# A hybrid decoder layer on one core: order of the first loads, a longer warm-up, and eight chunks at once for the first half of the tokens at the last gate

## The chip, the cores and the metric

The kernel runs on one core of a Trainium2 chip. The metric is the time of one execution on the device in microseconds (us). The kernel before has a median of 2290.51 us over 3 runs (2288.47 to 2292.35). One profiled execution of it took 2290.02 us, of which 2288.2 us are the span that the profile shows.

The engines: TensorE (PE in the profile) multiplies matrices, VectorE (DVE) and ScalarE (ACT) work on elements, SyncE (SP) issues transfers and computes nothing. ACT can issue transfers too. DMA engines move data between HBM and the on-chip memory SBUF. TensorE writes into PSUM, eight banks of 128 x 512 float32.

## What is computed

One decoder layer for 256 tokens of width 2048, in float32, cut to what matters here:

```python
h = layer_norm(alpha * x + 0.5 * swiglu(x, w_ffn1_gu, w_ffn1_down))      # first half-FFN
h = layer_norm(alpha * h + mixers(h))                                     # retention and windowed attention
h = layer_norm(alpha * h + 0.5 * swiglu(h, w_ffn2_gu, w_ffn2_down))      # second half-FFN
ple = sigmoid(h @ w_ple_gate) * (p @ w_ple_proj)                          # the last gate
out = layer_norm(alpha * h + ple)
def swiglu(x, w_gu, w_down):
    g, u = split(x @ w_gu, 2)
    return (silu(g) * u) @ w_down
```

The change touches the very first loads of the first half-FFN, and the seam between the second half-FFN (its last products with `w_ffn2_down`, then the layer norm) and the product with `w_ple_gate`, called the last gate below. In the kernel that weight is `w_pg`.

## The kernel before, in words

**Numbers in two parts.** Each float32 operand is split into a high part, rounded to the TensorE's float32r type by a copy on ACT, and a low part, the difference, made by DVE. The helper `split` (lines 92 to 94) does this. A product of two operands is three matmuls, low x high, high x high, high x low (`Sum.add`, lines 292 to 302).

**Chunks of weights.** Weights come in chunks of 512 KB, 128 x 1024 elements. A chunk needs a transfer into a raw buffer (`Chunk.__init__`, line 107), a copy on ACT (line 93) and a subtraction on DVE (line 94). The raw buffer is free after that, and the two parts are held until TensorE has used them. A chunk holds two blocks of 128 rows and 512 columns. Used for all 256 tokens it takes 12 matmuls: two halves of the tokens, t=0 and t=1, two row blocks, three matmuls each. This text calls the six matmuls of one chunk for one half of the tokens a *step*, and three of them, one row block, a *half-step*.

**The planner.** All chunks stand in `plan` in the order of their use. `fill()` (line 186), called whenever a chunk has been used, issues transfers (`load`) and conversions (`make`) for coming chunks. It makes the next loaded chunk while the chunks that are made and waiting amount to less than `room["ahead"]` (a chunk of this kind counts 12), loads while made and loaded ones amount to less than `room["far"]`, and does neither beyond `room["slots"]` buffers. `quiet(True)` stops conversions. All this happens when the program is written: it fixes the order of instructions on each engine, and every engine works in its order.

**The buffers.** Chunks, their parts, columns of the residual and other tiles of up to 4 KB a partition come from one pool of 46 buffers (`SLOTS`). An instruction that writes a new tile waits until the last reader of the buffer's previous tile is done. The framework hands buffers out in program order, and takes for each new tile the buffer that comes free first by its own plan.

**The end of the second half-FFN.** `ffn("f2", 2, ...)` works through the last half of the output columns in 19 units, plain pairs of chunks and units of seven products (`Seven`). After the last unit of seven, DVE folds four sums (`seven_common`, lines 405 to 408, then line 858). Six chunks, three each for output columns 2 and 3, are kept for the end: `held_out` runs their six steps for t=0, then their twelve half-steps for t=1. After the third step `Norm.columns` (in the profile as L907 and L539) adds a block to the residual and takes its statistics; after the sixth `Norm.normal(0)` does so for the last block, works out mean and variance and normalizes the first 512 columns of t=0 (lines 510 and 511). The rest of the norm is spread out: `turn((t, c))` normalizes columns c+1, transposes columns c on TensorE (line 518) and splits them into `ht`, the input of the last gate. Events (count, what) say after which half-step or step that happens; "sums" is `normal(1)`, the same for t=1.

**The last gate.** `embedding` multiplies `ht` with `w_pg` in four blocks of 512 columns, eight chunks each. Chunk c needs rows 2c and 2c+1 of `ht`, so two chunks for each `turn`. In block 0, `Norm.first` runs six chunks (`FRONT`) for t=0, then the same six for t=1, then two more for both halves. The four `ppr` tiles, p times its projection, are fetched at the start of the gate.

**The start.** `warm_up` has TensorE transpose the identity 14 times. `load_x_chunk(0)` issues the first quarter of x in three parts on SP, then the first two chunks of weights in two pieces each, one on ACT's queue, one on SP's.

The functions that the diff touches and what calls them, with the profile's line numbers:

Of the kernel before, what the change touches and what calls it, by code (L numbers as in the profile page):

```python
# [25 lines left out]
KD = D // P  # L26
# [3 lines left out]
HELD_MIX = 4  # L30
FRONT = 6

WARM = 14
FRONT_PAIRS = 3
HELD_PAIRS = 2, 3
SLOTS = 46
# [14 lines left out]
def layer(ctx: ExitStack, tc: tile.TileContext, io):  # L51
    nc = tc.nc
    sync, act, dve, pool, pe = nc.sync, nc.scalar, nc.vector, nc.gpsimd, nc.tensor
# [11 lines left out]
    def banks(name):  # L65
        return [bank(name + str(j)) for j in range(2)]

    def slot(shape, dt, name):
        return slots.tile(shape, dt, tag="slot", name=name)
# [116 lines left out]
    def fill(must=False):  # L186

        while True:
            queued = sum(u.time for u in ready)
            left = room["slots"] - room["used"]  # L190
            wanted = must and not ready or not room["quiet"] and queued < room["ahead"]
            if loaded and wanted and loaded[0].makes <= left:
                u = loaded.pop(0)
                u.make()
                room["used"] += u.keeps - u.loads
                ready.append(u)
                continue
            first = loaded[0] if loaded else plan[0] if plan else None
            queued += sum(u.time for u in loaded)
            if plan and queued < room["far"] and plan[0].loads + first.makes <= left:  # L200
                u = plan.pop(0)
                u.load()
                room["used"] += u.loads
                loaded.append(u)
                continue
            return
# [8 lines left out]
    def take(key):  # L215
        if not ready:
            fill(True)
        u = ready.pop(0)
        assert u.key == key, (u.key, key)
        return u  # L220

    def done(u):
        room["used"] -= u.keeps
        fill()

    def slots_for_weights(n, ahead=45, far=90):
        room.update(slots=n, ahead=ahead, far=far)
# [76 lines left out]
    def half_of(a, t):  # L304
        return tuple(x[:, t * P : (t + 1) * P] for x in a)

    def tokens_chunk(chunk, k0, lhs, sums, ts, kks=(0, 1)):
        for kk in kks:
            for t in ts:
                sums[t].add(half_of(lhs(k0 + kk), t), chunk.columns(kk))  # L310
# [419 lines left out]
    def gu_keys(name, j):  # L730
        return lambda n, p: (name + "_gu", j, n, p)
# [15 lines left out]
    def down_keys(name, b):  # L747
        return lambda n, p: (name + "_down", 2 * b + n, p)
# [9 lines left out]
    def ffn(name, i, ht, norm, keep, residual, keepers, away):  # L758
# [28 lines left out]
        for j in range(KF // 4):  # L787
# [9 lines left out]
            sums = [[Sum((pg, pu)[n][t], n_of[t, n]) for n in range(2)] for t in range(2)]  # L797
            got = []

            if norm is not None and j == 0:  # L800
                front, units = units[:FRONT_PAIRS], units[FRONT_PAIRS:]
                steps = [(gu_keys(name, 0)(n, p), 2 * p, n) for _, p in front for n in range(2)]
# [41 lines left out]
        lhs = lambda k: tuple(a[:, k % 4, :] for a in acts[k // 4])  # L844
# [9 lines left out]
        def fold(b):  # L854
            def f(*a):
                e, w = seven_common(*a)
                for x, v in ((y[2 * b], e), (y[2 * b + 1], w)):
                    dve.scalar_tensor_tensor(x, x, 2.0 * ALPHA, v, ALU.mult, ALU.add)
            return f
# [16 lines left out]
        sums = [[Sum(pn[n][t], n_of[0][t, n]) for n in range(2)] for t in range(2)]  # L876
# [5 lines left out]
            block_stats(stats, y, n)  # L882


        last_ahead = 136
        last = {}
        for at, (kind, p) in enumerate(second + [("P", p) for p in held]):
            last[p // 2] = at
# [11 lines left out]
        pt_ = [banks(f"{name}e{t}") for t in range(2)]  # L900
        sums = [[Sum(pt_[t][n], n_of[1][t, n]) for n in range(2)] for t in range(2)]
        block(f"{name}d1", second, down_keys(name, 1), lhs, forms, sums, fold(1), before_unit)
        slots_for_weights(27, last_ahead, last_ahead + 24)
        steps = [(down_keys(name, 1)(n, p), 2 * p, n) for n in range(2) for p in held]

        def combine(sl, p):
# [2 lines left out]
        norm = Norm((2, 3), sums, combine, y, stats, i, 4 * LN_EPS, keepers, away)  # L909
        if i < 2:  # L910
            events = ((8, (0, 0)), (10, (0, 1)), (11, (0, 2)), (12, "make"), (12, "make"), (12, "sums"))
            norm.run(steps, lhs, events, (0, 1), 4)
        else:
            norm.run(steps, lhs, ((8, (0, 0)), (11, (0, 1))))
        return norm


# [415 lines left out]
    def embedding(ht, norm, y):  # L1333
        stats = small.tile([P, 2, 4, 6], F32, tag="stats", name="plst", bufs=1)

        def finish(blk, ps, sg, t):
            sl = y[blk][:, t]
            act.activation(sg[:, t], ps, AF.Sigmoid)
            dve.tensor_tensor(sg[:, t], sg[:, t], pp[blk][:, t], ALU.mult)
            dve.scalar_tensor_tensor(sl, sl, ALPHA, sg[:, t], ALU.mult, ALU.add)  # L1340
            dve.bn_stats(stats[:, t, blk, :], sl)

        def last_norm(t, mv, rstd):
            rows = io["out"][0, t * P : (t + 1) * P]
            for c in range(4):
                ln_normal(y, t, mv, rstd, g, b, 4 * c, 4)
                at = slice(c * 512, c * 512 + 512)
                (act if t and c % 2 else sync).dma_start(rows[:, at], y[c][:, t])

        lhs = lambda k: (ht[:, k, :S], ht[:, k, S:])  # L1350
        for blk in range(4):
            pgs = banks(f"pg{blk}")
            sums = [Sum(b, KD) for b in pgs]
            sg = slot([P, 2, 512], F32, f"sg{blk}")
            key = ("w_pg", blk)
            if blk == 0:
                for j in range(4):
                    pp[j] = load_columns(pp, j, "ppr")
                steps = [(key + (c,), 2 * c, 0) for c in range(FRONT)]
                norm.first(steps, lhs, [[s] for s in sums], (  # L1360
                    (1, (0, 2)), (1, "sums"), (6, (1, 0)), (7, (1, 1)), (8, (0, 3)), (9, (1, 2)),
                    (10, (1, 3)), (10, "go"),
                ))
                slots_for_weights(24)
                for c in range(FRONT, KD // 2):
                    u = take(key + (c,))
                    tokens_chunk(u.chunk, 2 * c, lhs, sums, (0, 1))
                    done(u)
            elif blk < 3:
                for c in range(KD // 2):  # L1370
                    u = take(key + (c,))
                    tokens_chunk(u.chunk, 2 * c, lhs, sums, (0, 1))
                    done(u)
                    run_side()
            if blk < 3:
                finish(blk, pgs[0], sg, 0)
                later(1, lambda blk=blk, pgs=pgs, sg=sg: finish(blk, pgs[1], sg, 1))
                if blk == 0:
                    g, b = ln_vectors(3)
                continue  # L1380

            def first_done():
                finish(3, pgs[0], sg, 0)
                last_norm(0, *ln_stats(stats[:, 0], 3, 0, LN_EPS))

            steps = [(key + (c,), 2 * c, 0) for c in range(KD // 2)]
            held_out(steps, lhs, [[s] for s in sums], lambda t, j: None, first_done, lambda n: None, 0)
            finish(3, pgs[1], sg, 1)
            last_norm(1, *ln_stats(stats[:, 1], 3, 1, LN_EPS))
# [11 lines left out]
    def load_x_chunk(c):  # L1401
        raw = slot([P, 4, S], F32, f"xraw{c}")
        x_parts[c] = raw
        if c:
            sync.dma_start(raw, io["xT"][c])
            split_x(c, slice(0, 4))
            return
        parts = [slice(0, 1), slice(1, 2), slice(2, 4)]
        for at in parts:
            sync.dma_start(raw[:, at], io["xT"][c][:, at])  # L1410
        for queue in (act, sync):
            u = plan.pop(0)
            u.load(pieces=2, queue=queue)
            u.chunk.make_hi()
            room["used"] += u.keeps
            ready.append(u)
        first, second = (u.chunk for u in ready)
        split_x(c, parts[0])
        first.make_part(first.parts[0])
        split_x(c, parts[1])  # L1420
        first.make_part(first.parts[1])
        for at in second.parts:
            second.make_part(at)
        split_x(c, parts[2])

    def split_x(c, at):
        to = ht[:, 4 * c : 4 * c + 4, :][:, at]
        split(to[:, :, :S], to[:, :, S:], x_parts[c][:, at])

    def warm_up():  # L1430

        ps = bank("warm")
        for _ in range(WARM):
            pe.transpose(ps[:, :P], ident, ident)

    with tc.manual_schedule():
# [12 lines left out]
        norm = ffn("f1", 0, ht, None, x_parts, x_columns, (), rows[0])  # L1449
        norm = mixers(norm.new, norm, rows[0], kept, rows[1])  # L1450
        norm = ffn("f2", 2, norm.new, norm, norm.keep, rows[1], (), None)
# [102 lines left out]
```

## Time and profile before

| | us |
|---|---|
| median of 3 runs | 2290.51 |
| the runs | 2288.47, 2292.35, 2290.51 |
| the profiled execution | 2290.02 |
| its span | 2288.2 |
| TensorE busy in the span | 2268.8 (99%) |
| DVE busy | 1945.7 (85%) |
| ACT busy | 1184.7 (52%) |
| DMA, mean over the span | 204 GB/s |

A line of the timeline gives the start in us from the beginning of the span, the duration, the engine, the line of the kernel, what is written and read, and how many instructions are merged into it. In brackets stands how long the engine was idle before, and what released it. "SPq" and "ACTq" are issues of transfers; their time is that of the issue, not of the transfer. Starts of successive matmuls overlap: what counts is the distance from one start to the next.

### The profile page before, as it was taken

The numbers are of one execution on the slowest core, as the hardware profiler recorded it, in microseconds if no ns is written. First come the engines' busy times: TensorE is split into PE (matmuls) and PEld (weight loads), VectorE is DVE, ScalarE is ACT, GpSimd is POOL, SyncE is SP. The second block draws the span as 40 slices with busy tenths as digits, with TensorE's granted clock in tenths as the row PEclk, the third lists the DMA queues.
The fourth block names the chain that finished last, engine by engine and source line by source line (L and its number), as shares of the span: only waits on it lengthen the run. The fifth ranks groups of instructions, "written<-read, shape, count | busy, mean of one in ns | idle before, by whom it ended". The sixth has DMA issues, their size and how long they took to land.

```text
span 2288.2 us, 28790 instructions
## 1 busy us (share of the span) xinstructions
PE 2268.8 (99%) x10480; PEld 1883.5 (82%) x10480; DVE 1945.7 (85%) x2468; ACT 1184.7 (52%) x1427; POOL 95.5 (4%) x53
## 2 busy tenths in 40 slices
PE   9999999999999999999999999999999999999997
PEld 7888888888888888888778888888888888888876
DVE  7899999999888785677789786779999999889877
ACT  6555555556554342435556454355565555555532
POOL 0000000000000530124000000000000000000000
PEclk9999999999999999999999999999999999999999
DMA  8666665665577565555447567576666566565771
GB/s 298 199 206 195 198 211 180 206 200 192 214 279 278 179 222 169 166 165 163 140 150 243 167 224 274 190 233 206 197 189 208 184 201 216 181 220 194 276 276 55
DMA packets 193997, 465.83 MB, mean 204 GB/s; under 512 B 14784, under 2 KB 16448, under 8 KB 193856
## 3 DMA queue, kind: packets, MB, share of 16 engines
q1 hardware_dynamic: 191584, 460.91, 61.1%
q10 hardware_dynamic: 2272, 3.10, 0.5%
q8 instruction: 82, 1.34, 0.2%
q14 instruction: 59, 0.48, 0.1%
HBM read 455.56 MB, written 8.39 MB: 203 GB/s over the span
## 4 chain that ended last, share of the span: by engine, by line
PE 96%; DVE 3%; DMA 1%; issue 0%; ACT 0%; DVEq 0%; ACTq 0%
PE f1g L300 3%; PE f1g L302 3%; PE f1g L301 3%; PE f2g L302 3%; PE f2g L300 3%; PE f2g L301 3%; PE rqk L251 3%; PE f1u L300 2%; PE f1u L302 2%; PE f1u L301 2%; PE f2u L302 2%; PE f2u L300 2%; PE f2u L301 2%; PE aqk L251 2%; PE f2d L300 2%; PE f1d L300 2%
## 5 line engine op out<-in xcount | busy, mean ns | idle before, releaser
L94 DVE TENSOR_TENSOR lf_gu<-rf_gu,hf_gu 128x1024 fp32r<-128x1024 f32 (+1 forms) x284 | 334.5, 1212 | 14.4 <-ACT hf_gu L93 13.5
L93 ACT CAST hf_gu<-rf_gu 128x1024 fp32r<-128x1024 f32 (+1 forms) x284 | 282.3, 1043 | 18.8 <-DMA rf_gu<-in_f_gu 18.5
L94 DVE TENSOR_TENSOR lw_in_f<-rw_in_f,hw_in_f 128x1024 fp32r<-128x1024 f32 x140 | 195.7, 1428 | 29.4 <-ACT hw_in_f L93 26.8
L94 DVE TENSOR_TENSOR lf_down<-rf_down,hf_down 128x1024 fp32r<-128x1024 f32 x152 | 181.3, 1221 | 22.2 <-ACT hf_down L93 19.2
L93 ACT CAST hf_down<-rf_down 128x1024 fp32r<-128x1024 f32 x152 | 155.3, 1051 | 75.2 <-DMA rf_down<-in_f_down 21.4
L93 ACT CAST huf_gu<-uf_gu 128x1024 fp32r<-128x1024 f32 x70 | 73.7, 1054 | 158.0 <-DVE uf_gu L166 158.0
L93 ACT CAST hw_in_f<-rw_in_f 128x1024 fp32r<-128x1024 f32 x140 | 138.8, 1051 | 2.9 <-DMA rw_in_f<-in_w_in_f 2.7
L300 PE MATMUL f1g<-hf_gu,xt 128*128 128x512 f32 x247 | 97.2, 394 | 0.7 <-ACT hf_gu L93 0.7
L302 PE MATMUL f1g<-lf_gu,xt 128*128 128x512 f32 x247 | 97.1, 393 | 0.0
L301 PE MATMUL f1g<-hf_gu,xt 128*128 128x512 f32 x247 | 97.0, 393 | 0.0
L300 PE MATMUL f2g<-hf_gu,ht 128*128 128x512 f32 x247 | 96.3, 390 | 0.0
L302 PE MATMUL f2g<-lf_gu,ht 128*128 128x512 f32 x247 | 96.2, 389 | 0.0
L301 PE MATMUL f2g<-hf_gu,ht 128*128 128x512 f32 x247 | 96.1, 389 | 0.0
L93 ACT CAST hvf_gu<-vf_gu 128x1024 fp32r<-128x1024 f32 x70 | 73.8, 1055 | 29.7 <-DVE vf_gu L168 29.5
L829 ACT ACTIVATE eve<-eve 128x1024 f32<-128x1024 f32 x20 | 21.2, 1061 | 124.5 <-DVE eve L828 124.5
L94 DVE TENSOR_TENSOR luf_gu<-uf_gu,huf_gu 128x1024 fp32r<-128x1024 f32 x70 | 85.3, 1219 | 0.0
L94 DVE TENSOR_TENSOR lvf_gu<-vf_gu,hvf_gu 128x1024 fp32r<-128x1024 f32 x70 | 85.3, 1219 | 0.0
L300 PE MATMUL f2u<-hf_gu,ht 128*128 128x512 f32 x212 | 83.7, 395 | 0.0
L300 PE MATMUL f1u<-hf_gu,xt 128*128 128x512 f32 x212 | 83.4, 394 | 0.0
L302 PE MATMUL f2u<-lf_gu,ht 128*128 128x512 f32 x212 | 82.6, 390 | 0.0
L301 PE MATMUL f2u<-hf_gu,ht 128*128 128x512 f32 x212 | 82.6, 389 | 0.0
L301 PE MATMUL f1u<-hf_gu,xt 128*128 128x512 f32 x212 | 82.5, 389 | 0.0
(1336 smaller groups left out, 6432.0 us busy)
## 6 DMA issues: line engine op xcount, KB each, us to landing
rf_gu<-in_f_gu SPq DMA_DIRECT2D x350, 512.0 KB, 4.9
rf_down<-in_f_down SPq DMA_DIRECT2D x176, 512.0 KB, 4.4
rw_in_f<-in_w_in_f SPq DMA_DIRECT2D x148, 512.0 KB, 4.4
rw_rv<-in_w_rv SPq DMA_DIRECT2D x32, 512.0 KB, 4.5
rw_ret<-in_w_ret SPq DMA_DIRECT2D x32, 512.0 KB, 4.7
rw_mix<-in_w_mix SPq DMA_DIRECT2D x32, 512.0 KB, 4.4
rw_pg<-in_w_pg SPq DMA_DIRECT2D x32, 512.0 KB, 4.6
rw_att<-in_w_att SPq DMA_DIRECT2D x16, 512.0 KB, 4.6
```

The source lines that it names most:

```text
L93: act.copy(dst_hi, src)
L94: (lo_engine or dve).tensor_tensor(dst_lo, src, dst_hi, ALU.subtract)
L251: pe.matmul(ps[f], hi[:, kk, f * P : (f + 1) * P], rhs(k), start=k == 0, stop=k == n_k - 1,)
L300: pe.matmul(o, al, bh, start=first, stop=False)
L301: pe.matmul(o, ah, bh, start=False, stop=False)
L302: pe.matmul(o, ah, bl, start=False, stop=self.left == 0)
L829: act.activation(g, g, AF.Silu)
```

## The change

There are four edits. (1) At the start both first chunks of weights go on SP's queue, in the order chunk 0, chunk 1; the first two parts of x go on ACT's queue, the third on SP's behind the weights. (2) `WARM` goes from 14 to 17. (3) In the second half-FFN alone, `last_ahead` goes from 136 to 160 and the slots at the held chunks from 27 to 31, and `turn((0, 0))` and `turn((0, 1))` come after half-steps 9 and 12 in place of 8 and 11. (4) Block 0 of the last gate runs all eight chunks for t=0 and then all eight for t=1; the events are moved accordingly, and `turn((0, 3))` now comes before "sums".

```diff
-WARM = 14
+WARM = 17
...
-        last_ahead = 136
+        last_ahead, n_ahead = (136, 27) if i < 2 else (160, 31)
...
-        slots_for_weights(27, last_ahead, last_ahead + 24)
+        slots_for_weights(n_ahead, last_ahead, last_ahead + 24)
...
-            norm.run(steps, lhs, ((8, (0, 0)), (11, (0, 1))))
+            norm.run(steps, lhs, ((9, (0, 0)), (12, (0, 1))))
...
-                steps = [(key + (c,), 2 * c, 0) for c in range(FRONT)]
+                steps = [(key + (c,), 2 * c, 0) for c in range(KD // 2)]
                 norm.first(steps, lhs, [[s] for s in sums], (
-                    (1, (0, 2)), (1, "sums"), (6, (1, 0)), (7, (1, 1)), (8, (0, 3)), (9, (1, 2)),
-                    (10, (1, 3)), (10, "go"),
+                    (1, (0, 2)), (2, (0, 3)), (2, "sums"), (7, (1, 0)), (9, (1, 1)), (11, (1, 2)),
+                    (12, (1, 3)), (12, "go"),
                 ))
                 slots_for_weights(24)
-                for c in range(FRONT, KD // 2):
-                    u = take(key + (c,))
-                    tokens_chunk(u.chunk, 2 * c, lhs, sums, (0, 1))
-                    done(u)
...
         parts = [slice(0, 1), slice(1, 2), slice(2, 4)]
-        for at in parts:
-            sync.dma_start(raw[:, at], io["xT"][c][:, at])
-        for queue in (act, sync):
+        for j in range(2):
             u = plan.pop(0)
-            u.load(pieces=2, queue=queue)
+            u.load(pieces=2, queue=sync)
             u.chunk.make_hi()
             room["used"] += u.keeps
             ready.append(u)
+            for at in (parts[:2], parts[2:])[j]:
+                (sync if j else act).dma_start(raw[:, at], io["xT"][c][:, at])
```

## The prediction

> **What bounds the kernel now.** I read the page first, then what TensorE waited for, then the timeline of the two places that the change touches.
>
> ```profile
> PE 2268.8 (99%) x10480; PEld 1883.5 (82%) x10480; DVE 1945.7 (85%) x2468; ACT 1184.7 (52%) x1427; POOL 95.5 (4%) x53
> ```
>
> TensorE is the bound. All its waits of the whole execution fit in one answer:
>
> ```profile
> PE warm L1434 <- POOL ident masks.py:199: 1.4, 1, 1.4
> PE pg L300 <- DVE ht L94: 1.3, 1, 1.3
> PE lnps L518 <- DVE f1y L511: 1.0, 2, 0.5
> PE f1g L300 <- ACT hf_gu L93: 0.7, 1, 0.7
> PE lnps L518 <- DVE f2y L511: 0.5, 2, 0.3
> PE lnps L518 <- DVE mixy L511: 0.3, 1, 0.3
> ```
>
> The change can reach 0.7 (first matmul) and 1.3 + 0.5 (last gate): 2.5 us of waits. The timeline of TensorE at the start adds a slow clock:
>
> ```profile
> 1.36 3.25 PE L1434 MATMUL warm<-ident 128*128 128x128 f32 x14 [1.36 <-POOL ident masks.py:199]
> 5.28 0.79 PE L300 MATMUL f1g<-hf_gu,xt 128*128 128x512 f32 x1 [0.67 <-ACT hf_gu L93]
> ...
> 9.71 0.63 PE L301 MATMUL f1g<-hf_gu,xt 128*128 128x512 f32 x1
> 10.14 0.63 PE L302 MATMUL f1g<-lf_gu,xt 128*128 128x512 f32 x1
> 10.56 0.46 PE L300 MATMUL f1u<-hf_gu,xt 128*128 128x512 f32 x1
> 10.86 0.39 PE L301 MATMUL f1u<-hf_gu,xt 128*128 128x512 f32 x1
> ```
>
> Matmuls start 0.427 apart until 10.56, then 0.227: half speed, and full speed from about 10.73 (the step between the last two lines, 0.30, mixes both).
>
> At the last gate DVE sets the pace. Its timeline, the six conversions of gate chunks 0 to 5 behind it, and two starts on TensorE:
>
> ```profile
> 2166.03 1.22 DVE L858 SCALAR_TENSOR_TENSOR f2y<-f2y,evw 128x1024 f32<-128x1024 f32 x1
> 2167.16 4.66 DVE L94 TENSOR_TENSOR lw_pg<-rw_pg,hw_pg 128x1024 fp32r<-128x1024 f32 x4
> 2171.74 0.68 DVE L907 TENSOR_TENSOR f2y<-f2y,f2e 128x512 f32<-128x512 f32 x1
> ...
> 2177.88 0.48 DVE L511 SCALAR_TENSOR_TENSOR f2y<-f2y,rstd,ln_b 128x256 f32<-128x256 f32 x1
> ...
> 2178.42 0.44 PE L518 MATMUL lnps<-ident,f2y 128*128 128x128 f32 x2 [0.30 <-DVE f2y L511]
> ...
> 2192.96 0.50 PE L300 MATMUL pg<-hw_pg,ht 128*128 128x512 f32 x1 [1.32 <-DVE ht L94]
> ```
>
> The reader is to see that four low parts (1.145 each) stand right before the first statistics (L907), that DVE has no gap between them, and that TensorE's first turn waits for what follows.
>
> **Edit 1, the queues.** First weights are issued at 0.74 (SP's first slot) in place of 0.90 on ACT, x at 0.90 in place of 0.74. x was converted from 3.05, so now from 3.2, still ahead of the weights' 4.61, which become about 4.45. Seven transfers as before, five on SP and two on ACT; chunks behind them move by no issue. The third x part falls behind two pieces of chunk 1; it was converted at 8.36 and is used at 13.38, three chunks in, so it stays covered. Gain 0.15 us at most, if TensorE is free.
>
> **Edit 2, three more transposes.** 14 took 3.25, so three take about 0.7: they fill the gap 4.61 to 5.28 and the first matmul cannot come much before 5.1. What they buy is the clock, if an unbroken stretch is what raises it. Nothing in the trace shows that, so bounds: no gain; or the whole slow stretch of 5.45 us (12.8 matmuls) at 0.227, 2.55 us saved. I take 0.9 for edits 1 and 2 together, between 0.1 and 2.7. If it is gained, chunk 2 is late next: its low part was ready at 11.66 and TensorE would want it near 11.7.
>
> The end of the trace shows the opposite change: the last matmul starts at 2273.71 and the clock halves at about 2277.15. The row is one half microsecond: busy time of PE, PEld, DVE, ACT and POOL, the granted clock (0.65, full before and 0.50 after), the DMA share and GB/s.
>
> ```profile
> 2277.00:2277.50 0.50, 0.00 (x0) 0.00 (x0) 0.43 (x3) 0.00 (x0) 0.00 (x0) 0.65 0.00 0
> ```
>
> [...]
>
> **Edit 3, more chunks made ahead.** By the planner's count, made chunks stand at 132 or 144 against 136 when the held chunks begin: six gate chunks. Against 160 they reach 168: eight. The two extra conversions come after the fold (L858) and ahead of L907 on DVE. Two low parts cost 2.3 us of DVE (two rows of 1.145) where it has no gap. The two ACT copies (1.05 each) lie in ACT's idle time before 2178.
>
> Worse are their buffers. Before, the transfer of chunk 7 took the last buffer that was free by the plan; the next tiles, the four ppr, got what half-steps 2 and 4 of t=1 release, and the transfers were issued only then (t=1 begins at 2172.28, half-steps end at 2173.6 and 2175.0):
>
> ```profile
> 2173.62 0.33 SPq L623 DMA_DIRECT2D ppr<-ppd  x1
> ...
> 2174.98 0.32 SPq L623 DMA_DIRECT2D ppr<-ppd  x1
> ```
>
> Now high part 6 takes that free buffer, and low part 6, the transfer of 7 and both parts of 7 stand where ppr stood. So DVE, at the latest free at 2172, waits for low part 6 until 2173.6. Transfer 7 is issued at about 2173.7; chunks 2 to 4 needed 3.7 to 4.2 from issue to copy (2158.66 to 2162.83, 2161.38 to 2165.11, 2164.10 to 2167.93), so 2177.5. Copy to 2178.6, low part to 2179.8. L907 comes at 2179.8 in place of 2171.74: 8.1 late, and everything behind it in DVE's order with it: the norm of t=0, the first turns, and on TensorE the half-steps behind them. Bounds: 2.3 us if buffers are there, 2.7 with chunk 7's landing, 5.5 if only the parts wait (low part 7 at 2176.1 to 2177.25), 8.1 as worked out, 9 with the median landing of 4.6.
>
> The later events, half-steps 9 and 12, give TensorE 0.68 more before each turn: worth the 0.30 and 0.25 of waits above if nothing else moved.
>
> **Edit 4, eight steps for t=0.** No matmul is added or dropped. Two more steps (2 x 1.365 = 2.73) cover the chain of t=1. But "sums" now stands behind the low part of turn (0, 3), which needs a transpose after step 2: from transposes to low part done took 1.94 (2194.46 to 2196.40). Event by event, with durations of the rows:
>
> - Without edit 3's delay L907 of t=1 would start 1.4 later than 2185.81, and TensorE, two steps further, would meet its result with 0.1 of wait in place of 1.3.
> - With 2.3 to 2.7 us more on DVE, TensorE waits 2.1 at the first turn and some 0.3 at each of three more, and starts t=1 at 2196.7 to 2197. Eight steps, three turns at 0.47 and 0.15 for the second turn's low part end block 0 at 2209.1 to 2209.5; before it ended at 2208.6. Cost 0.5 to 0.9.
> - With 8.1, half-step 9 ends at 2178.42 as before and the first turn is ready at 2185.6: TensorE idles 7.0 us, twice the 3 us after which the clock fell at the end. Second transposes at 2186.5, then half-steps 10 to 12 at 0.427 a matmul to 2190.5, second turn to 2191.2, step 1 to 2192.9, step 2 to 2194.6, low part of (0, 3) at 2196.5, L907 of t=1 10.6 late, t=1 at 2203.6, end of block 0 at 2216.1: 7.5 late, 6.3 if the clock stays up. Chunks 0 to 7 of block 1 are converted long before; no work of TensorE is left to win that back.
>
> **Sum against the profiled execution** (2290.02, 0.49 under the median): minus 0.9, plus 7.5: 2296.6.
>
> **Rivals.**
> - *The buffers are there in time* (not slower). Speaks for it: the planner counts at most 31 of its slots. Against: raws wait for DVE in the plan, and ppr shows no other buffer free. Place: transfer 7. Decides: issued before about 2168, it lands by 2172. Gate 0.9 late: 2290.02 - 0.9 + 0.9 = 2290.0.
> - *Only the parts wait*, transfer 7 goes early: DVE 5.5 late, 3.2 us above the 0.5 case, 3.7: 2292.8.
> - *The gate gains*: the extra low parts fit ahead of the fold, where DVE waited 1.3 us for a copy, and TensorE's 1.8 of waits mostly go: gate -1.5, start -1.7: 2286.8. Against: their order on DVE is behind the fold.
> - *The warm-up buys nothing*: only 0.1 from the start, 2297.4, with the buffer case. In every case the clock may rise no sooner.
>
> [...]
>
> **How the numbers follow.** Full buffer wait 0.66, only the parts 0.10, buffers in time 0.16, gate gains 0.08; the warm-up that buys nothing 0.45 within each. The likeliest alone reaches from 2294.0 (clock stays up, start gives 2.3) to 2298.8 (median landing, start gives nothing). The range takes in the buffers in time: 2289.6 to 2298.8. 0.2% of the median, about what a measurement of this kernel can tell from no change, is 4.6 us, so slower begins at 2295.1 and faster at 2285.9. The full wait lies above 2295.1 in 85 of 100, 0.56, plus 0.01 of the parts: slower 0.57. Faster needs gate and clock at their best: 0.03. Same 0.40.
>
> **What would show it.** Right: a transfer of gate chunk 7 issued after 2173; two more L94 rows before L907; L907 some 8 us later; TensorE's longest wait at the first turn, 5 to 8 us, with a dip of its clock behind it; one pitch of 0.227 earlier than 10.7 at the start if the transposes count. Wrong: transfer 7 issued with 6, L907 under 3 us late; or a start that gains more than 2.7.

## The result and the profile after

The changed kernel has a median of 2296.07 us over 7 runs (2295.41 to 2298.02), beside 2289.91 us for the kernel before on the same chip (7 runs, 2288.28 to 2292.35). The ratio is 1.0029, with a 95% interval of 1.0019 to 1.0039: slower by 6.2 us. The profiled execution took 2298.02 us, the slowest of the seven, of which 2296.2 us are the span; that is 8.0 us above the profiled execution of before.

The first line of the page is that of the engines' busy time. TensorE is busy 2.7 us longer than before, with three more transposes and some slower matmuls:

```profile
PE 2271.5 (99%) x10483; PEld 1885.8 (82%) x10483; DVE 1945.1 (85%) x2468; ACT 1184.8 (52%) x1427; POOL 95.9 (4%) x53
```

All waits of TensorE in the changed kernel (the total in us, how many, the longest one):

```profile
PE lnps L518 <- DVE f2y L511: 7.1, 2, 6.9
PE warm L1430 <- POOL ident masks.py:199: 1.4, 1, 1.4
PE lnps L518 <- DVE f1y L511: 1.2, 3, 0.5
PE f1g L300 <- ACT hf_gu L93: 0.6, 1, 0.6
PE lnps L518 <- DVE mixy L511: 0.3, 1, 0.3
```

Two readings matter. The wait of 1.3 us for `ht` where t=1 began at the last gate is gone, as edit 4 promises. In its place the first turn of norm 2 waits 6.9 us for DVE, where it waited 0.3 before. The timeline around that wait, with the lines of DVE, of the transfers (SPq), of ACT and of TensorE in order of time:

```profile
2165.61 1.22 DVE L858 SCALAR_TENSOR_TENSOR f2y<-f2y,evw 128x1024 f32<-128x1024 f32 x1
2166.74 3.49 DVE L94 TENSOR_TENSOR lw_pg<-rw_pg,hw_pg 128x1024 fp32r<-128x1024 f32 x3
2171.80 1.23 DVE L94 TENSOR_TENSOR lw_pg<-rw_pg,hw_pg 128x1024 fp32r<-128x1024 f32 x1 [1.57 <-ACT hw_pg L93]
2173.86 1.23 DVE L94 TENSOR_TENSOR lw_pg<-rw_pg,hw_pg 128x1024 fp32r<-128x1024 f32 x1 [0.84 <-PE f2e L301]
2174.03 0.33 SPq L107 DMA_DIRECT2D rw_pg<-in_w_pg  x1
...
2177.61 1.05 ACT L93 CAST hw_pg<-rw_pg 128x1024 fp32r<-128x1024 f32 x1 [4.57 <-DMA rw_pg<-in_w_pg]
2178.69 1.22 DVE L94 TENSOR_TENSOR lw_pg<-rw_pg,hw_pg 128x1024 fp32r<-128x1024 f32 x1 [3.61 <-ACT hw_pg L93]
2179.83 0.68 DVE L907 TENSOR_TENSOR f2y<-f2y,f2e 128x512 f32<-128x512 f32 x1
...
2185.69 0.66 PE L518 MATMUL lnps<-ident,f2y 128*128 128x128 f32 x2 [6.93 <-DVE f2y L511]
2186.51 0.69 PE L518 MATMUL lnps<-ident,f2y 128*128 128x128 f32 x2 [0.17 <-DVE f2y L511]
```

Six low parts of gate chunks now stand between the fold (L858) and L907, where there were four. The fifth in this list, of chunk 6, is released by a matmul of the half-steps (`<-PE f2e L301`): it waited for a buffer. Then the transfer of chunk 7 is issued at 2174.03, its copy runs at 2177.61, and DVE stands idle for 3.61 us until it can make the low part. L907 starts at 2179.83 in place of 2171.74, and the first turn on TensorE at 2185.69.

The idle time costs speed too: behind it half-steps 10 to 12 run at 0.427 a matmul, where in the kernel before matmuls start 0.23 apart in this stretch. In the windows view a row is a stretch of time: its length, busy time of PE, PEld, DVE, ACT and POOL, the granted clock, the DMA share and GB/s. In the changed kernel the clock falls within the wait (at about 2181.47) and is full again only from about 2191.68:

```profile
2181.00:2182.00 1.00, 0.00 (x0) 0.00 (x0) 0.97 (x3) 0.00 (x0) 0.00 (x0) 0.72 0.58 213
2190.00:2191.00 1.00, 1.00 (x4) 0.70 (x3) 0.96 (x2) 0.00 (x0) 0.00 (x0) 0.50 1.01 401
2191.00:2192.00 1.00, 1.00 (x7) 0.96 (x6) 0.33 (x1) 0.11 (x1) 0.00 (x0) 0.66 1.03 414
```

At the start, the timeline of TensorE in the changed kernel:

```profile
1.36 3.89 PE L1430 MATMUL warm<-ident 128*128 128x128 f32 x17 [1.36 <-POOL ident masks.py:199]
5.85 0.76 PE L300 MATMUL f1g<-hf_gu,xt 128*128 128x512 f32 x1 [0.60 <-ACT hf_gu L93]
...
10.25 0.54 PE L301 MATMUL f1g<-hf_gu,xt 128*128 128x512 f32 x1
10.63 0.39 PE L302 MATMUL f1g<-lf_gu,xt 128*128 128x512 f32 x1
```

and, from its chain of waits, two of the steps ahead of that first matmul (start, duration, what):

```profile
0.91 3.91 DMA xraw<-in_xT
...
4.84 0.41 ACT xt L93
```

The gap ahead of the first matmul is still there, and the first matmul comes at 5.85 in place of 5.28, because the first part of x takes 3.91 us from its issue on ACT's queue, and ACT copies the first weights only behind it. In this execution the clock rises at about 10.6, hardly sooner than before (10.73).

To compare kernels at the last gate I use the *last stretch*: from the start of the first matmul of t=1's twelve half-steps to the start of the kernel's last matmul. It holds the same products in all kernels. Before, it is 2172.30 to 2273.71, 101.41 us; after, 2172.47 to 2281.71, 109.24 us: 7.83 of the 8.0 us lie there. A TensorE that reaches this stretch early can make it longer (102.87 us with edits 1 and 2 alone, whose gate is that of before), so where the stretches of two kernels are compared, their starts count too.

In the table below, one execution each of two kernels (7131 us with low parts 6 and 7 on POOL, 4665 us with six chunks made ahead) lies far from all others and is left out of the median.

### The profile page after: what moved, and what is told of

Its sections match the earlier page's. It is cut to its first block, busy times and chain, and to the rows that moved or that the text cites. A ratio compares the mean times of both kernels' runs of the same rounds, so it can differ in the third digit from the quotient of the medians.

```text
span 2296.2 us, 28792 instructions
## 1 busy us (share of the span) xinstructions
PE 2271.5 (99%) x10483; PEld 1885.8 (82%) x10483; DVE 1945.1 (85%) x2468; ACT 1184.8 (52%) x1427; POOL 95.9 (4%) x53
## 4 chain that ended last, share of the span: by engine, by line
PE 97%; DVE 2%; DMA 1%; ACT 0%; issue 0%; ACTq 0%
PE f1g L300 3%; PE f1g L301 3%; PE f1g L302 3%; PE f2g L302 3%; PE f2g L300 3%; PE f2g L301 3%; PE rqk L251 3%; PE f1u L301 2%; PE f1u L300 2%; PE f1u L302 2%; PE f2u L302 2%; PE f2u L300 2%; PE f2u L301 2%; PE aqk L251 2%; PE f2d L300 2%; PE f1d L300 2%
## 5 line engine op out<-in xcount | busy, mean ns | idle before, releaser
L301 PE MATMUL f1g<-hf_gu,xt 128*128 128x512 f32 x247 | 97.0, 393 | 0.0
L301 PE MATMUL f2g<-hf_gu,ht 128*128 128x512 f32 x247 | 96.1, 389 | 0.0
L301 PE MATMUL f2u<-hf_gu,ht 128*128 128x512 f32 x212 | 82.6, 390 | 0.0
L301 PE MATMUL f1u<-hf_gu,xt 128*128 128x512 f32 x212 | 82.6, 389 | 0.0
```

Source lines behind the costliest of these rows:

```text
L301: pe.matmul(o, ah, bh, start=False, stop=False)
```

## The experiments

Times are medians; "before" is the kernel before on the same chip. The last column is the last stretch of the profiled execution.

| kernel | us | before | ratio (95%) | last stretch |
|---|---|---|---|---|
| after | 2296.07 | 2289.91 | 1.0029 [1.0019, 1.0039] | 109.24 |
| edits 3 and 4 alone | 2296.33 | 2289.95 | 1.0027 [1.0016, 1.0037] | 109.16 |
| edits 1 and 2 alone | 2289.41 | 2289.95 | 0.9997 [0.9988, 1.0006] | 102.87 |
| three buffers freed | 2290.45 | 2289.95 | 1.0002 [0.9994, 1.0011] | 103.49 |
| transfer 7 first | 2293.42 | 2289.95 | 1.0015 [1.0006, 1.0024] | 105.81 |
| clock kept up | 2295.27 | 2289.50 | 1.0024 [1.0015, 1.0033] | 107.91 |
| low parts 6, 7 on POOL | 2290.56 | 2289.50 | 1.0004 [0.9995, 1.0013] | 103.81 |
| edit 2 alone | 2288.56 | 2289.50 | 0.9995 [0.9986, 1.0004] | 102.48 |
| edit 1 alone | 2290.00 | 2289.50 | 1.0001 [0.9992, 1.0010] | 102.26 |
| after without edit 4 | 2298.07 | 2289.55 | 1.0034 [1.0021, 1.0046] | 110.53 |
| after, six chunks made ahead | 2294.03 | 2289.55 | 1.0018 [1.0009, 1.0027] | none |
| seven chunks, low part 6 on POOL | 2288.54 | 2289.55 | 0.9995 [0.9986, 1.0004] | 101.60 |
| seven chunks, low part 6 on DVE | 2290.60 | 2289.55 | 1.0004 [0.9995, 1.0012] | 103.84 |

### The gate's edits and the start's edits apart

**Edits 3 and 4 alone.** The start is that of before.

```diff
-WARM = 17
+WARM = 14
...
-        for j in range(2):
+        for at in parts:
+            sync.dma_start(raw[:, at], io["xT"][c][:, at])
+        for queue in (act, sync):
             u = plan.pop(0)
-            u.load(pieces=2, queue=sync)
+            u.load(pieces=2, queue=queue)
```

> The kernel after with the start of the kernel before (14 transposes, weights and x on the queues as before): edits 3 and 4 alone. Theory (the buffers hold transfer 7 and the low parts of chunks 6 and 7): the whole loss is here, block 0 of the gate ends 7 to 8 us later than before, TensorE's longest wait is 6.5 to 7.5 at the first turn, time 7 to 8 us above before. Rival (the start costs part of the 6.2): the wait at the first turn stays but the time is only 4 to 5 us above before.

**Edits 1 and 2 alone.** The gate is that of before.

```diff
-WARM = 14
+WARM = 17
...
-        for at in parts:
-            sync.dma_start(raw[:, at], io["xT"][c][:, at])
-        for queue in (act, sync):
+        for j in range(2):
             u = plan.pop(0)
-            u.load(pieces=2, queue=queue)
+            u.load(pieces=2, queue=sync)
...
+            for at in (parts[:2], parts[2:])[j]:
+                (sync if j else act).dma_start(raw[:, at], io["xT"][c][:, at])
```

> The kernel before with edits 1 and 2 alone. [...] Rival (the longer warm-up pays): 1.5 to 2.5 us faster, full speed before 8 us.

Measured: 2296.33, which is 6.4 above before (7 to 8 were expected), and 2289.41, 0.5 below. The whole loss lies in edits 3 and 4; their last stretch is 109.16, as in the changed kernel. The start's edits can't be told from nothing in time, but their profile holds a surprise: the gap is there, and yet the clock rises sooner. The timeline of TensorE in the kernel with edits 1 and 2 alone:

```profile
1.36 3.71 PE L1434 MATMUL warm<-ident 128*128 128x128 f32 x17 [1.36 <-POOL ident masks.py:199]
5.71 0.47 PE L300 MATMUL f1g<-hf_gu,xt 128*128 128x512 f32 x1 [0.64 <-ACT hf_gu L93]
6.01 0.40 PE L301 MATMUL f1g<-hf_gu,xt 128*128 128x512 f32 x1
```

The same 17 transposes take 3.71 in place of 3.89, and the very first matmul runs at full speed (it lasts 0.47, in the changed kernel 0.76): here the clock rose during the transposes. TensorE then reaches t=1's half-steps at 2170.20, 2.10 us ahead of before. But its last matmul starts at 2273.07, only 0.64 ahead, because L907 of t=0 moves only from 2171.74 to 2171.12: the copy of gate chunk 5 waits for its transfer, and DVE waits 1.53 us for that copy. So 1.46 of the 2.10 us that TensorE had won are given back here.

**Edit 1 alone**, the kernel before with the second part of the diff just shown, and **edit 2 alone**, the kernel before with its first part:

```diff
-WARM = 14
+WARM = 17
```

> The kernel before with the new queues and its 14 transposes. Theory (x on ACT's queue lands late beside weights on SP's): the first copy of x at 4.6 to 4.9 in place of 3.05, the first matmul at 5.6 to 5.9 with 1.0 to 1.2 us of wait behind the transposes; the start loses 0.3 to 0.6 and the time is 2290.2 to 2290.5. Rival (x lands by the order of issue, 0.15 later): the first copy at 3.2, first matmul at 5.1, 2289.8.

> The kernel before with 17 transposes and its old queues. The transposes end at about 5.25 and the first matmul starts near 5.28: TensorE has no gap. [...]

Edit 1 alone: the first copy of x starts at 4.70 (3.05 before), the first matmul at 5.71 behind 1.10 us of wait, as the theory of the late x said; 2290.00 is 0.5 above before, which its interval does not tell from nothing. Edit 2 alone, in the timeline of TensorE:

```profile
1.36 3.89 PE L1434 MATMUL warm<-ident 128*128 128x128 f32 x17 [1.36 <-POOL ident masks.py:199]
5.36 0.79 PE L300 MATMUL f1g<-hf_gu,xt 128*128 128x512 f32 x1
...
6.38 0.63 PE L302 MATMUL f1g<-lf_gu,xt 128*128 128x512 f32 x1
6.80 0.45 PE L300 MATMUL f1g<-hf_gu,xt 128*128 128x512 f32 x1
7.09 0.40 PE L301 MATMUL f1g<-hf_gu,xt 128*128 128x512 f32 x1
```

There is no gap, and the clock rises at about 6.9, before at 10.73; the first f1u matmul starts at 8.91 in place of 10.56. t=1's half-steps begin at 2170.44, 1.86 ahead; 0.79 of it is left at the last matmul, 2272.92. The median is 0.9 below before. In its profile edit 2 does what it says, and the profiles with edit 1 show the gap again. In time neither can be told from nothing.

### What the gate waits for

**Three buffers freed.** The changed kernel, but norm 2 fetches one vector and uses it for all four halves of its gain and shift. The output is then not the layer's; all work on the engines stays, and three transfers of 512 KB, near 2130 in the other kernels, are left out.

```diff
     def ln_vectors(i):
+        if i == 2:
+            v = slot([P, 1024], F32, "ln_g2_0")
+            sync.dma_start(v, io["ln_g"][0, i : i + 1, 0:1024].broadcast_to([P, 1024]))
+            return [v, v], [v, v]
```

> The kernel after, but the norm behind the second half-FFN takes one tile of 1024 gains for all its gains and shifts, which leaves three of four vectors unloaded (its numbers are therefore not those of the layer) and three buffers free. Instructions of DVE, ACT and TensorE are the same. Theory: transfer 7 goes out with 6 before 2167, the low parts of 6 and 7 follow without the long wait, L907 starts at 2173 to 2175 in place of 2179.8, the first turn waits 0.5 to 2.5 in place of 6.9, the clock stays up, and the time is within 1.5 us of before (0.2 to 1.5 above). Rival (the two conversions as DVE work, or the new order of the passes, cost it): still 5 us or more above before.

**Transfer 7 first.** The changed kernel, but the transfer of gate chunk 7 is issued before the parts of chunk 6 take their buffers.

```diff
             left = room["slots"] - room["used"]
+            if plan and plan[0].key == ("w_pg", 0, 7) and loaded and left >= 1:
+                u = plan.pop(0)
+                u.load()
+                room["used"] += u.loads
+                loaded.append(u)
+                continue
```

> The kernel after, but the transfer of chunk 7 stands before the parts of chunk 6, so that it takes the buffer that is free early; the parts of 6 and 7 then all wait for half-steps 2 and 4 of the second pass. Theory: L907 at about 2177.2 in place of 2179.8, the first turn waits about 4.3 in place of 6.9, time 3.5 to 5 us above before; the difference to the kernel after, 2.5 to 3.5, is the price of the late transfer. Rival (the transfer is not what ends last): as the kernel after, 6 to 7.5 above before.

With three more buffers the loss is nearly gone: 2290.45, 0.5 above before. All eight low parts are still made ahead of the first statistics. The transfers that are left out stood some 40 us ahead of the wait, so the buffers and not the traffic are the likely cause; the next kernel leaves out none. The timeline of DVE and TensorE in that kernel (L911 is what L907 was, L522 what L518 was):

```profile
2170.01 1.22 DVE L94 TENSOR_TENSOR lw_pg<-rw_pg,hw_pg 128x1024 fp32r<-128x1024 f32 x1 [1.01 <-ACT hw_pg L93]
2171.88 1.23 DVE L94 TENSOR_TENSOR lw_pg<-rw_pg,hw_pg 128x1024 fp32r<-128x1024 f32 x1 [0.65 <-PE f2e L301]
2173.02 0.68 DVE L911 TENSOR_TENSOR f2y<-f2y,f2e 128x512 f32<-128x512 f32 x1
...
2178.88 0.41 PE L522 MATMUL lnps<-ident,f2y 128*128 128x128 f32 x2 [2.11 <-DVE f2y L515]
```

The copy of chunk 7 now runs at 2170.20, and only its low part still waits 0.65 us for a buffer. The statistics start at 2173.02.

With transfer 7 first the parts still wait for buffers. The last two copies on ACT are now held by half-steps, no longer by a transfer. In its timeline (L913 is what L907 was):

```profile
2172.38 1.05 ACT L93 CAST hw_pg<-rw_pg 128x1024 fp32r<-128x1024 f32 x1 [2.37 <-PE f2e L307]
2173.74 1.06 ACT L93 CAST hw_pg<-rw_pg 128x1024 fp32r<-128x1024 f32 x1 [0.30 <-PE f2e L307]
...
2175.97 0.68 DVE L913 TENSOR_TENSOR f2y<-f2y,f2e 128x512 f32<-128x512 f32 x1
```

2293.42 us: of the 6.2 us that were lost, the late transfer is 2.65 (2296.07 less 2293.42), and the parts that wait for buffers about 3.0 (2293.42 less 2290.45). 0.5 is left as the net of all the rest: the work of two more low parts on DVE, and the low part of chunk 7 that still waits 0.65 us, less what the other edits win.

### Whose order it is

**Low parts 6 and 7 on POOL.** The changed kernel; buffers, transfers and steps stay where they are.

```diff
         def make(self):
             self.make_hi()
-            split(self.hi, self.lo, self.raw)
+            split(self.hi, self.lo, self.raw, pool if self.key in (("w_pg", 0, 6), ("w_pg", 0, 7)) else None)
```

> The changed kernel with the low parts of gate chunks 6 and 7 made by POOL in place of DVE; every buffer, transfer and step stays where it is. Theory (the loss is DVE standing at those two low parts for their buffers, with L907 behind them in its order): L907 starts when the low part of chunk 5 is done, 2171.7 to 2173.0 in place of 2179.8, although transfer 7 is still issued near 2174; TensorE's wait at the first turn falls from 6.9 to under 1.5 us, and the time to between 2288.3 and 2290.5. A low part of 128x1024 takes POOL some 4 us by its rows of 128x512 (1.9 to 2.3), so that of chunk 7 is done by 2184, ahead of its use. Rival (it is the late transfer or the slots themselves that hold the gate, not DVE's order): L907 stays near 2179.8 and the time at 2296. Rival (POOL is slower beside DVE and TensorE waits for low part 7 in its eight steps): 2291 to 2293.

2290.56 us, at the upper end of what was expected (2290.5). Transfer 7 goes out at 2172.12, 1.9 earlier than in the changed kernel, as is TensorE itself in this execution, and L907 starts at 2171.68, ahead even of that: nothing but DVE's own order tied it to chunks 6 and 7. But TensorE still waits 2.75 us at the first turn, more than expected. The timeline of DVE and POOL shows why:

```profile
2172.00 2.40 POOL L94 TENSOR_TENSOR lw_pg<-rw_pg,hw_pg 128x1024 fp32r<-128x1024 f32 x1 [1094.77 <-PE f2e L301]
2173.01 0.67 DVE L907 TENSOR_TENSOR f2y<-f2y,f2e 128x512 f32<-128x512 f32 x1
...
2176.39 0.48 DVE L510 SCALAR_TENSOR_TENSOR f2y<-f2y,mv,ln_g 128x256 f32<-128x256 f32 x1
2176.83 2.34 POOL L94 TENSOR_TENSOR lw_pg<-rw_pg,hw_pg 128x1024 fp32r<-128x1024 f32 x1 [2.43 <-ACT hw_pg L93]
2176.91 2.54 DVE L511 SCALAR_TENSOR_TENSOR f2y<-f2y,rstd,ln_b 128x256 f32<-128x256 f32 x1
2179.37 0.47 DVE L510 SCALAR_TENSOR_TENSOR f2y<-f2y,mv,ln_g 128x256 f32<-128x256 f32 x1
```

Beside POOL's first low part L907 runs at its usual 0.67. Beside the second, an instruction of DVE that takes 0.48 lasts 2.54: it ends at 2179.45, POOL's low part at 2179.17. The 2.06 us that it loses on the path are what the theory had left out.

**Seven chunks, low part 6 on POOL, and the same on DVE.** The kernel before with 17 transposes, seven chunks made ahead, seven steps for t=0, and late turns in norm 2; the two differ in the engine of one low part.

```diff
-        last_ahead = 136
+        last_ahead, n_ahead = (136, 27) if i < 2 else (150, 29)
...
-                steps = [(key + (c,), 2 * c, 0) for c in range(FRONT)]
+                steps = [(key + (c,), 2 * c, 0) for c in range(7)]
...
-                    (1, (0, 2)), (1, "sums"), (6, (1, 0)), (7, (1, 1)), (8, (0, 3)), (9, (1, 2)),
-                    (10, (1, 3)), (10, "go"),
+                    (1, (0, 2)), (1, "sums"), (5, (0, 3)), (6, (1, 0)), (8, (1, 1)), (10, (1, 2)),
+                    (11, (1, 3)), (11, "go"),
...
-            split(self.hi, self.lo, self.raw)
+            split(self.hi, self.lo, self.raw, pool if self.key == ("w_pg", 0, 6) else None)
```

> The kernel before with 17 transposes (old queues), seven gate chunks made ahead (150, 29 slots), seven steps for t=0 with the turn of (0, 3) behind step 5, turns of norm 2 at half-steps 9 and 12, and the low part of chunk 6 made by POOL. Theory (POOL holds DVE only where DVE reads two operands from SBUF, and here it works beside L907, which reads PSUM): L907 of t=0 starts at 2170.9 to 2171.8, TensorE does not wait at the start of t=1 (1.3 before), the gate ends 0.8 to 1.2 earlier, the start gives some 0.9 more: 2287.3 to 2288.0. Rival (POOL's low part falls on the norm's two-operand instructions and holds them up to 2 us, as the low part of chunk 7 did): 2288.6 to 2289.6.

> The same with the low part of chunk 6 on DVE, nothing else changed. Theory (DVE stands at that low part for the buffer that half-step 2 of t=1 frees): L907 of t=0 at 2173.0 to 2175.0, TensorE waits 2 to 3.5 us at the first turn; 2289.3 to 2291.0, 1.5 to 3 us above the one with POOL. Rival (the buffer is free early enough by TensorE's head start): as with POOL plus one low part, 1.2 us.

On DVE, 2290.60. The low part of chunk 6 waits for the buffer that a half-step frees, and L907 comes behind it, in the expected range:

```profile
2172.11 1.23 DVE L94 TENSOR_TENSOR lw_pg<-rw_pg,hw_pg 128x1024 fp32r<-128x1024 f32 x1 [1.66 <-PE f2e L301]
2173.25 0.68 DVE L907 TENSOR_TENSOR f2y<-f2y,f2e 128x512 f32<-128x512 f32 x1
```

On POOL, 2288.54, lower by 2.06, with L907 at 2171.14. TensorE no longer waits where t=1 begins. But the gain of 0.8 to 1.2 at the gate is not there: the last stretch is 101.60, as before. The timeline of POOL and DVE in that kernel:

```profile
2172.93 2.40 POOL L94 TENSOR_TENSOR lw_pg<-rw_pg,hw_pg 128x1024 fp32r<-128x1024 f32 x1 [1094.79 <-PE f2e L301]
2173.18 0.69 DVE L539 BATCH_NORM_STATS2 f2st<-f2y 128x6 f32<-128x512 f32 x1
...
2174.20 1.13 DVE L461 SCALAR_TENSOR_TENSOR nv<-mv,cst 128x2 f32<-128x2 f32 x1
```

Beside POOL's low part (2172.93 to 2175.33) the statistics keep their 0.69, but a two-operand instruction on two elements takes 1.13 in place of 0.16, up to POOL's end. So the rival of this run was right in its mechanism, with 1.0 us of its 2. Neither this kernel nor edit 2 alone beats the kernel before by more than the measurement can tell: both have 0.9995 with an interval of 0.9986 to 1.0004.

### The clock in the wait

**Clock kept up.** The changed kernel with 62 more transposes of the identity behind half-step 9, written to a bank that nobody reads.

```diff
+                if what == "busy":
+                    ps = bank("busy")
+                    for _ in range(62):
+                        pe.transpose(ps[:, :P], ident, ident)
...
-            norm.run(steps, lhs, ((9, (0, 0)), (12, (0, 1))))
+            norm.run(steps, lhs, ((9, "busy"), (9, (0, 0)), (12, (0, 1))))
```

> The changed kernel with 62 more transposes of the identity on TensorE behind half-step 9, ahead of the first turn, into a bank of PSUM of their own; at some 0.107 us each at the full clock they fill about 6.6 of the 6.9 us in which TensorE waits. Theory (transposes count as work for the clock, as the start of the run with edits 1 and 2 alone shows it): the granted clock stays at 1.00 from 2181 to 2192, half-steps 10 to 12 run at 0.227 a matmul, L907 stays at 2179.8, and of the 7.5 to 8.0 us that the gate lost 1.0 to 1.3 come back: 2294.9. Rival (transposes do not count): the clock falls and rises as before, 2296.1, or later by what the transposes delay the turn. Rival (the wait moves on behind the faster half-steps): the clock holds and the time still stays at 2296.

The timeline of TensorE in that kernel, and two rows of its windows:

```profile
2177.50 6.93 PE L571 MATMUL busy<-ident 128*128 128x128 f32 x62
2184.58 0.44 PE L518 MATMUL lnps<-ident,f2y 128*128 128x128 f32 x2 [0.15 <-DVE f2y L511]
```

```profile
2181.00:2182.00 1.00, 1.00 (x12) 1.00 (x11) 0.93 (x3) 0.00 (x0) 0.00 (x0) 1.00 1.02 414
2190.00:2191.00 1.00, 0.94 (x7) 0.63 (x6) 1.00 (x3) 0.00 (x0) 0.00 (x0) 1.00 1.01 401
```

The clock stays full (1.00 in both rows, where the changed kernel has 0.72 and 0.50), half-steps 10 to 12 run at 0.23 a matmul, and the last stretch is 107.91, 1.33 shorter than 109.24. So these 62 transposes kept the clock up, and the slow clock behind the wait costs 1.3 us of the 7.8 in the profile. The time does not confirm the size: 2295.27 is 5.8 above its own before, the changed kernel 6.2, and their intervals overlap.

### Edit 3 and edit 4 apart

**After without edit 4.** Eight chunks made ahead, but block 0 of the gate as before.

```diff
-                steps = [(key + (c,), 2 * c, 0) for c in range(KD // 2)]
+                steps = [(key + (c,), 2 * c, 0) for c in range(FRONT)]
...
-                    (1, (0, 2)), (2, (0, 3)), (2, "sums"), (7, (1, 0)), (9, (1, 1)), (11, (1, 2)),
-                    (12, (1, 3)), (12, "go"),
+                    (1, (0, 2)), (1, "sums"), (6, (1, 0)), (7, (1, 1)), (8, (0, 3)), (9, (1, 2)),
+                    (10, (1, 3)), (10, "go"),
...
+                for c in range(FRONT, KD // 2):
+                    u = take(key + (c,))
+                    tokens_chunk(u.chunk, 2 * c, lhs, sums, (0, 1))
+                    done(u)
```

> The changed kernel without edit 4: all eight gate chunks are still made ahead, but t=0 takes six steps and the events at the gate are those of the kernel before. Theory (edit 3 alone is the loss, and edit 4 wins a little of it back): L907 of t=0 stays near 2179.8 and TensorE's wait at the first turn near 6.9; L907 of t=1 needs no turn of (0, 3) first and comes about 1.7 earlier than 2196.8, but six steps no longer cover the chain behind it, so TensorE waits some 1.4 us where t=1 begins and the last two chunks are behind it: block 0 ends near 2218.0 in place of 2216.65, 2297.4. Rival (edit 4 costs or is worth nothing): 2296.1 or less.

2298.07 us, the slowest of all. L907 of t=0 starts at 2179.24 and TensorE waits 6.86 us, so the wait belongs to edit 3 alone. The wait that edit 4 removes is back, in the timeline of TensorE:

```profile
2201.77 0.50 PE L300 MATMUL pg<-hw_pg,ht 128*128 128x512 f32 x1 [1.29 <-DVE ht L94]
```

The last stretch is 110.53, 1.29 longer than in the changed kernel: by the profiles edit 4 is worth 1.3 us here, as expected. By the times it is worth 2.4 (8.5 above before against 6.2), with intervals that overlap. So with chunks 6 and 7 made ahead edit 4 is a gain, and edit 3 costs several times as much.

**After, six chunks made ahead.** The changed kernel with the planner's numbers of before.

```diff
-        last_ahead, n_ahead = (136, 27) if i < 2 else (160, 31)
+        last_ahead, n_ahead = 136, 27
```

> The changed kernel with the planner's numbers of before (136 and 27 slots): six gate chunks are made ahead, the low parts of 6 and 7 are made on the way through the eight steps. Theory: L907 of t=0 goes back to 2171.5 to 2172.2 and the long wait of TensorE falls from 6.9 to under 1.2. What is lost instead: the low parts of 6 and 7 now stand on DVE among the norm of t=1, so steps 7 and 8 of t=0 wait for them, 1 to 1.5 us each. Time 2290.2 to 2291.5. Rival (the eight steps themselves are the loss): 2294 to 2296.

2294.03 us, a miss of 2.5 above the upper end of the theory; the time lies in the range of the rival, by which the eight steps themselves are the loss. Taking back the making ahead while keeping the eight steps wins about 2 of the 6.2 us; 4.5 us above before are left. So edit 4 needs edit 3: without chunks 6 and 7 made ahead the eight steps lose more than they cover.

In the profile of this kernel a matmul of 128x512 lasts 0.67 us on average, 0.39 in that of before, so its waits cannot be set beside the others. The order of the instructions can. From its timeline of ACT and TensorE, at the eighth step:

```profile
4484.20 0.82 ACT L93 CAST ht<-lnps 128x256 fp32r<-128x256 f32 x2 [13.02 <-PE lnps L518]
4484.91 1.05 ACT L93 CAST hw_pg<-rw_pg 128x1024 fp32r<-128x1024 f32 x1
4486.01 0.70 PE L300 MATMUL pg<-hw_pg,ht 128*128 128x512 f32 x1 [1.41 <-ACT hw_pg L93]
```

Conversions are stopped by `quiet` until "go", so chunk 7 is converted only where its step asks for it. Its copy then stands on ACT behind the first turn of t=1, so the eighth step, which was to cover the norm of t=1, comes after that norm. The theory had placed the low parts of 6 and 7 among that norm, at 1 to 1.5 us a step, but not this copy behind the turn. That this makes up the rest of the 4.5 us is not shown: no profile of this kernel at the speed of the others exists.

## Why the prediction was right

The predicted 2296.6 lies 0.5 above the median, and slower was the likeliest case. The mechanism at the gate is the one that was forecast; that the number is so close is in part luck, as told below. One sum of the prediction does not come out: with the median landing and no gain at the start, its own terms (2290.02, 7.5, and 0.9 for a landing that ends at 9 in place of 8.1) give 2298.4, not 2298.8.

**Edit 3, the buffers: right, event by event.** By the steps of the prediction, with what the profile shows: low part of 6 at 2173.6 (2173.86); transfer 7 issued at 2173.7 (2174.03); its copy at 2177.5 (2177.61); L907 at 2179.8 (2179.83); TensorE idle for 7.0 (6.93); first turn at 2185.6 (2185.69), second pair of transposes at 2186.5 (2186.51); half-steps 10 to 12 at half speed, 0.427 a matmul, to 2190.5 (2190.84); L907 of t=1 10.6 late (10.96, from 2185.81 to 2196.77). The gate was to be 7.5 late; the last stretch is 7.83 longer. That the buffers are the cause, and not the work of two more low parts, is shown by the kernel with three buffers freed, 0.5 above before, and by that with transfer 7 first, which has the same work and lost 2.65 less.

**The two rivals on the same path were well sized.** "Only the parts wait" gave 2292.8; with transfer 7 first, 2293.42. "The buffers are there in time" gave 2290.0; with three buffers freed, 2290.45.

**The clock: right in the profile.** 1.2 us were set for the dip (7.5 against 6.3); the kernel that keeps the clock up has a last stretch that is 1.33 shorter. The times alone (5.8 against 6.2 above before) would not show it.

**Edits 1 and 2: wrong in one step, and too large.** The step "x was converted from 3.05, so now from 3.2" failed: it was converted from 4.84. The order of the issues did not decide it; the part of x issued at 0.91 on ACT's queue took 3.91 us beside four pieces of weights on SP's, where the same part, first on SP's queue, took 2.3 (issue 0.74, copy 3.05). Whether the other queue or the weights issued ahead of it made it late, no run separates. With it "they fill the gap" fell too: 0.60 us of it is left. The sum took 0.9 for the two edits together; the profile shows 0.17 lost by t=1's half-steps (2172.47 against 2172.30), and the medians a gain of 0.5 (edits 1 and 2 alone) and 0.3 (the changed kernel against edits 3 and 4 alone), none of which can be told from zero.

**A miss that cancelled.** In the profile the gate costs 7.8 and the start 0.2, 8.0 together, against 6.6 predicted (7.5 less 0.9). The median is only 6.2 above before. So by the profiled executions, from which it was worked out, the forecast is 1.4 too low, and beside the median it is 0.5 too high; that nearness is luck. The profiled execution is the slowest of the seven, and its clock rose at 10.6, where it rises sooner in four of the six profiles with 17 transposes that are set out below. Also, the clock is down for 10.2 us both in the profile of the changed kernel and in that without edit 4 (2181.09 to 2191.33), which has the same long wait; where the dip lies in the other executions no profile shows, and the 1.3 us that it costs may be less there. That is an argument, not shown.

**The transposes and the clock.** The prediction left it open whether transposes raise the clock. The runs show that these did: 62 of them held it at 1.00 through the wait, where it fell to 0.50 without them, and in two profiles the clock rose while the 17 of the warm-up still ran (last section). In the profile both appear as plain MATMUL rows in float32.

## What to carry to other kernels

When a planner makes more tiles ahead, count buffers and not only engine time: the loss is set by which earlier tile's last reader frees the buffer, and it reaches everything that stands behind that conversion in the order of its engine. Look up where the next tiles in the profile get their buffers (here the four `ppr` transfers, issued only at 2173.6 and 2175.0); these rows, with the time that a chunk takes to land, foretold 8.1 us. Time won early in a kernel is not kept unless the last seam can use it: of 2.1 us of lead 0.64 reached the end. And two edits can need each other: here the eight steps win with chunks 6 and 7 made ahead, and lose without them.

## What the runs showed of the hardware that was not expected

**The rise of the clock at the start differs from kernel to kernel, and it mostly came sooner with 17 transposes.** It is read here from the distance between the starts of matmuls, 0.427 before and 0.227 after. Of the kernels with 14 transposes, all three profiles (before, edits 3 and 4 alone, edit 1 alone) have the clock full only at 9.7 to 10.7. Of six profiles with 17 transposes, two run the first matmul at full speed (edits 1 and 2 alone, behind a gap of 0.64, and seven chunks with low part 6 on POOL, without one): it lasts 0.47 and 0.50, in the other four 0.76 to 0.80. In these two the row of the transposes itself is shorter (3.71 and 3.84 in place of 3.89), so the rise lies inside it. Two more, both without a gap (edit 2 alone, seven chunks with low part 6 on DVE), rise at about 6.9, and two, both with a gap of 0.5 to 0.6 (the changed kernel, after without edit 4), at 10.2 to 10.6. Fourteen transposes last 3.25 us, seventeen 3.89 where the clock does not rise among them. Why the same 17 raise it in one kernel 3.3 us or more sooner than in another, no run shows.

**Two instructions of DVE lasted as long as POOL's subtraction beside them.** Beside POOL's subtraction of two SBUF tiles, two instructions of DVE with two operands in SBUF took far longer than elsewhere and ended with it or shortly after (0.48 became 2.54, to 2179.45, with POOL done at 2179.17; 0.16 became 1.13, to 2175.33, as POOL's), while L907, which reads one operand from PSUM, and the statistics, which read one tile, kept their 0.67 and 0.69. What held the two no run shows. POOL's own low part of 128x1024 took 2.34 to 2.40 us, not the 4 that its rows of half the size had let me expect.
